# Strassen's seven products in the FFN up-projection of a one-core hybrid decoder layer

## The chip, the cores and the metric

The kernel runs on one core of one Trainium2 chip. The core has five engines with queues of their own, each strictly in order: TensorE (PE in the profile; its weight loads are PEld), VectorE (DVE), ScalarE (ACT), GpSimd (POOL) and SyncE (SP), which here only issues DMAs. They share one on-chip memory, SBUF. TensorE writes its sums to PSUM, of which the FFN uses eight banks; here VectorE and ScalarE read them. The metric is the device time of one execution in microseconds (us).

## The reference

One layer of a hybrid decoder for 2048 prompt tokens and 8 x 4 sample tokens (2080 columns in all), everything in float32. Sliding-window attention and a state space model run side by side, are normed, merged and projected; then comes a gated feed-forward network (FFN) with a short convolution in it:

```
def _conv_ffn(h, prev, w_up, conv_w, conv_b, w_down):
    L = h.shape[1]
    up = h @ w_up
    buf = jnp.concatenate([prev.astype(up.dtype), up], axis=1)
    c = conv_b + sum(conv_w[i] * buf[:, i:i + L] for i in range(CONV_W))
    a, g = jnp.split(c, 2, axis=-1)
    return (jax.nn.silu(g) * a) @ w_down, buf[:, -(CONV_W - 1):]
```

`h` has 1024 features, `up` has 2 x 2688 (value half and gate half), the convolution is three tokens wide, and `w_down` leads back to 1024 features. A last norm follows. The sample tokens have their own past rows `prev`, and the last rows of `up` are returned.

## The kernel before, in words

Features lie on the 128 partitions, tokens along the free axis. Each float32 operand of a large matrix product is split into a high part with float32r's bits and the exact rest (`split`: ScalarE casts the high part, line 85; GpSimd or VectorE subtracts it from the source, line 88). A product is three matmuls per 128 x 128 weight block: high x high, high x low, low x high (`mm3`, lines 93 to 95).

The FFN is the last stage, 760 us to the end. It goes over three groups of two token tiles (some 346 columns each, and two columns of context); for each group over 21 pairs of 128 value and 128 gate features (j = 0 to 20). For each j the weights `wur` (two blocks of 128 x 1024) are loaded and split into `wuh` and `wul`, and `w_down`'s 128 rows into `wdh` and `wdl`. `up(ti, j, ws)` then multiplies: for each half 8 feature blocks x 3 matmuls into one PSUM bank, tag `up`, of which there are four. The convolution reads that bank: ScalarE writes cc = w2 x + b (line 1185), VectorE adds the other two taps (lines 1186 and 1187, one input in PSUM, one in SBUF), ScalarE takes the silu of the gate (1204), VectorE multiplies value and gate (1205, both inputs in SBUF), and the result is split into `ah`, `al`. After every third j, `down` multiplies those with w_down in 16 PSUM banks (tag `dn`, three buffers), and VectorE adds each to the running sum `acc` (1223). The down sums are queued in `todo` and issued after a later `up`, so that the activations are ready.

The order on each engine is set when the program is built: a tile scheduler lists the instructions of each engine once, from the order of the code and priorities, and puts semaphores where a tile is reused. At run time each engine takes its own list from the top. A buffer of a tag with n buffers is free for the (n+1)th tile only when the first has been read for the last time. For the FFN these numbers matter: `wur` 2, `wuh` and `wul` 3, `wdh` and `wdl` 4, `ah` and `al` 7, `up` 4 banks, `dn` 3 banks.

## Time and profile before

| what | value |
|---|---|
| time, median of 3 runs | 2242.93 us (2241.89 to 2244.98) |
| span of the profiled execution | 2245.1 us |
| TensorE busy, matmuls | 2137.4 us, 14183 |
| VectorE, ScalarE, GpSimd busy | 1237.0, 930.8, 978.1 us |
| first and last start of an up matmul | 760.1 and 2206.1 us |
| up and down matmuls of the FFN | 6048 and 3024 |
| mean granted TensorE clock | 0.984 |

A row of a group reads: line, engine, operation, output <- inputs (buffer numbers left out), shapes, count | busy us in all, mean ns of one | idle time of the engine just before them, and what ended it. A matmul's duration is longer than the distance to the next one, because matmuls are pipelined; the distance is read from counts in a full stretch. Timeline rows give the start in us from the span's start, the duration, the engine and the instruction.

### The profile page before, as it was taken

The page shows a single profiled execution, that of the slowest core. Times are in us where ns is not written, and L with a number is a line of the kernel's source. Part 1 is how long each engine was busy: PE and PEld are TensorE (multiplying, and loading weights), DVE is VectorE, ACT ScalarE, POOL GpSimd, SP SyncE. Part 2 cuts the span into 40 slices and gives each one's busy share as a digit, 9 for nine tenths or more (in the row PEclk, how much of TensorE's full clock was granted, in tenths as well). Part 3 has the DMA queues.
Part 4 walks back from the last instruction along what each step waited for, and adds up shares of the span by engine and source line. Part 5 has one row for each costly group of instructions (what it writes and reads, how often), then busy time and mean ns, then how long its engine had stood idle before and what let it go on. Part 6 is the DMA issues. An engine that isn't in the chain of part 4 may idle for free.

```text
span 2245.1 us, 37919 instructions
## 1 busy us (share of the span) xinstructions
PE 2137.4 (95%) x14183; PEld 2068.2 (92%) x14183; DVE 1237.0 (55%) x2786; ACT 930.8 (41%) x1970; POOL 978.1 (44%) x1044
## 2 busy tenths in 40 slices
PE   8969999978999999999999899999999999999997
PEld 8967878857999999999998899999999999999997
DVE  8859898357677654444443654333335743333335
ACT  6526554764444434333333632332224532233333
POOL 4857775343444134433334333443325443344332
PEclk9989999989999999999999999999999999999999
DMA  7765434786365632222126442222213422122202
GB/s 232 240 166 144 137 104 125 144 239 197 114 193 180 207 128 85 81 71 66 48 76 82 136 139 63 85 69 73 69 45 123 142 78 72 40 85 85 66 29 52
DMA packets 204807, 253.22 MB, mean 113 GB/s; under 512 B 32952, under 2 KB 177216, under 8 KB 204608
## 3 DMA queue, kind: packets, MB, share of 16 engines
q1 hardware_dynamic: 204624, 250.80, 39.1%
q8 instruction: 112, 1.84, 0.4%
q14 instruction: 71, 0.58, 0.1%
HBM read 188.69 MB, written 57.71 MB: 110 GB/s over the span
## 4 chain that ended last, share of the span: by engine, by line
PE 63%; DVE 1%; DMA 1%; ACT 1%; issue 0%; POOL 0%; DVEq 0%; ACTq 0%
PE up L95 14%; PE up L94 14%; PE up L93 14%; PE dn L94 7%; PE dn L93 7%; PE dn L95 7%; DMA h2s<-h2scr 1%; DVE acc L1238 0%; PE wo L94 0%; PE wo L95 0%; PE wo L93 0%; DVE cc L1205 0%; DVE h2l L88 0%; DVE acc L1223 0%; ACT h2h L85 0%
## 5 line engine op out<-in xcount | busy, mean ns | idle before, releaser
L95 PE MATMUL up<-h2h,wul 128*128 128x348 f32 (+1 forms) x2016 | 651.0, 323 | 1.4 <-POOL wul L88 1.4
L93 PE MATMUL up<-h2h,wuh 128*128 128x348 f32 (+1 forms) x2016 | 648.6, 322 | 1.4 <-ACT cc L1192 1.4
L94 PE MATMUL up<-h2l,wuh 128*128 128x348 f32 (+1 forms) x2016 | 649.9, 322 | 0.0
L1186 DVE SCALAR_TENSOR_TENSOR cc<-up,cw,cc 128x346 f32<-128x346 f32 (+1 forms) x252 | 144.0, 572 | 456.9 <-ACT cc L1185 456.9
L93 PEld LDWEIGHTS up<-h2h,wuh 128*128 128x128 f32 x2016 | 380.2, 189 | 2.1 <-ACT cc L1192 1.7
L95 PEld LDWEIGHTS up<-h2h,wul 128*128 128x128 f32 x2016 | 380.4, 189 | 1.7 <-POOL wul L88 1.7
L94 PEld LDWEIGHTS up<-h2l,wuh 128*128 128x128 f32 x2016 | 378.5, 188 | 0.4
L88 POOL TENSOR_TENSOR wul<-wur,wuh 128x1024 fp32r<-128x1024 f32 x122 | 294.1, 2411 | 151.5 <-ACT wuh L85 145.8
L93 PE MATMUL dn<-ah,wdh 128*128 128x346 f32 (+1 forms) x1008 | 324.9, 322 | 12.9 <-DVE acc L1223 12.9
L94 PE MATMUL dn<-al,wdh 128*128 128x346 f32 (+1 forms) x1008 | 325.7, 323 | 0.7 <-POOL al L88 0.7
L95 PE MATMUL dn<-ah,wdl 128*128 128x346 f32 (+1 forms) x1008 | 324.4, 322 | 0.0
L1223 DVE TENSOR_TENSOR acc<-acc,dn 128x346 f32<-128x346 f32 (+1 forms) x336 | 172.8, 515 | 230.6 <-PE dn L95 229.8
L88 POOL TENSOR_TENSOR wdl<-wdr,wdh 128x1024 fp32r<-128x1024 f32 x62 | 149.2, 2421 | 345.0 <-PE dn L95 329.9
L88 POOL TENSOR_TENSOR al<-cc,ah 128x346 fp32r<-128x346 f32 (+1 forms) x126 | 118.4, 940 | 340.1 <-ACT ah L85 335.2
L1185 ACT ACTIVATE cc<-up,cw 128x346 f32<-128x346 f32 (+1 forms) x252 | 159.3, 633 | 130.3 <-PE up L95 125.0
L85 ACT CAST wdh<-wdr 128x1024 fp32r<-128x1024 f32 x63 | 64.3, 1048 | 339.9 <-PE dn L94 320.8
L93 PEld LDWEIGHTS dn<-ah,wdh 128*128 128x128 f32 x1008 | 191.7, 190 | 14.4 <-DVE acc L1223 14.3
L94 PEld LDWEIGHTS dn<-al,wdh 128*128 128x128 f32 x1008 | 191.1, 190 | 1.1 <-POOL al L88 1.0
L95 PEld LDWEIGHTS dn<-ah,wdl 128*128 128x128 f32 x1008 | 191.9, 190 | 0.0
L85 ACT CAST wuh<-wur 128x1024 fp32r<-128x1024 f32 x126 | 132.2, 1050 | 132.0 <-PE up L94 126.8
L94 PE MATMUL wo<-ml,wo 128*128 128x260 f32 x512 | 147.3, 288 | 2.4 <-POOL ml L88 1.8
L93 PE MATMUL wo<-mh,wo 128*128 128x260 f32 x512 | 149.1, 291 | 0.3 <-ACT mh L85 0.2
(405 smaller groups left out, 4133.5 us busy)
## 6 DMA issues: line engine op xcount, KB each, us to landing
wur<-in_w_up SPq DMA_DIRECT2D x126, 512.0 KB, 3.6
wdr<-in_w_down SPq DMA_DIRECT2D x63, 512.0 KB, 4.1
x<-in_xT SPq DMA_DIRECT2D x56, 256.0 KB, 3.8
mt<-mscr SPq DMA_DIRECT2D x16, 520.0 KB
xm<-in_xT SPq DMA_DIRECT2D x64, 130.0 KB, 3.0
x2scr<-xm SPq DMA_DIRECT2D x64, 130.0 KB, 2.0
h2scr<-h SPq DMA_DIRECT2D x64, 130.0 KB, 2.6
loscr<-hl_p SPq DMA_DIRECT2D x28, 256.0 KB, 4.4
```

What stands on the lines that cost most here:

```text
L85: nc.scalar.copy(hi, src)
L88: lo_eng.tensor_tensor(lo, src, hi.bitcast(F32), ALU.subtract)
L93: nc.tensor.matmul(ps, w[0], x[0], start=first, stop=False)
L94: nc.tensor.matmul(ps, w[0], x[1], start=False, stop=False)
L95: nc.tensor.matmul(ps, w[1], x[0], start=False, stop=last)
L1185: nc.scalar.activation(cp, pp[:, 2:], AF.Identity, bias=w[3], scale=w[2])
L1186: nc.vector.scalar_tensor_tensor(cp, pp[:, 1 : npr + 1], w[1], cp, ALU.mult, ALU.add)
L1223: nc.vector.tensor_tensor(x[:, m, :n], x[:, m, :n], pt[:, :n], ALU.add)
```

## The change

The FFN's up-projection of one j is a 2 x 2 block product: two feature halves of the weights (value v, gate g) against two token tiles, each cut into two halves of 512 features. It is now done in seven products of 512 features (Winograd's form of Strassen's algorithm) where it had been eight. A product is 4 feature blocks x 3 matmuls of 348 or 350 columns.

- The right-hand sums and differences of the tokens (`x0`, `q0`, `q1`, `t2`) are built once per group in `load_first` and `load_rest`: four VectorE operations for each of four feature blocks, and splits.
- The left-hand sums of the weights are built for every j in `load_wup`: `s1` = g1 + g2 and the first half of `s24` on VectorE, the second half of `s24` and g1 = v1 - g1 (in place) on GpSimd. Then 3.5 blocks of 1024 columns (tags v, s, g, t) are split where it had been 2. The low parts are GpSimd's.
- `unit` runs the seven products. Four of them add up one after another in one PSUM bank (`ux`, two buffers); after each of the first three ScalarE copies the running sum out (c11, c12, u3), and the chain's next product waits for that copy. The other three (u2, u3, u4) go to two banks of tag `up` and are added by VectorE, which also makes the two differences. Of the four results three now lie in SBUF (c11 and c21 in tile `ca`, c12 in `cb`), one in PSUM.
- `conv` does the convolution of a tile as before, but reads those results.
- `down` runs after every second j (11 times a group, before 7), between the fourth and fifth product of the unit that follows the pair. It is called the middle sum below.
- Buffers: `wdh`, `wdl` 3 (before 4), `ah`, `al` 5 (before 7), tiles of 350 columns, `wur` 2 and `wuh`, `wul` 3 as before, though a unit now uses four of the latter and not two. The samples' tails go out by two small DMAs per j, their past rows come by one.

```diff
-TILESF = [(0, 316, NSMP)] + [(348 + 346 * i, 346, 0) for i in range(4)] + [(1732, 348, 0)]
+TILESF = [(0, 316, NSMP), (348, 348, 0)] + [(696 + 346 * i, 346, 0) for i in range(4)]
-AB, WB = 7, 4
+AB, WB, DB_, CB = 5, 3, 2, 6
+SQ = (1, 1)
-        psu, psu_close = psum("fpu", 4)
+        psx, psx_close = psum("fpx", 2)
+        psu, psu_close = psum("fpu", 2)
...
+            for k in range(4):
+                b0 = stage(c2, "c2", gi, 0, k, 4, "hb0")
+                b1 = stage(c2, "c2", gi, 1, k, 4, "hb1")
...
+                v.tensor_tensor(b11, b12, b11, ALU.subtract)
+                v.tensor_tensor(t2, b22, b11, ALU.subtract)
+                v.tensor_tensor(b12, b22, b12, ALU.subtract)
+                v.tensor_tensor(b21, b21, t2, ALU.subtract)
...
+            def pair(src, nm):
+                n = src.shape[1]
+                h = wp.tile([P, KD, P], F32R, tag="wuh", name=f"wh{nm}_{gi}_{j}", bufs=3)[:, 0:n]
+                l = wp.tile([P, KD, P], F32R, tag="wul", name=f"wl{nm}_{gi}_{j}", bufs=3)[:, 0:n]
+                split(nc, h, l, src, nc.scalar, lo_eng)
+                return [[t[:, i : i + 4] for t in (h, l)] for i in range(0, n, 4)]
+            a11, a12 = pair(v, "v")
...
+            nc.vector.tensor_tensor(s1, g[:, 0:4], g[:, 4:8], ALU.add)
+            nc.vector.tensor_tensor(s24[:, 0:4], s1, v[:, 0:4], ALU.subtract)
+            (nc.vector, nc.gpsimd)[SQ[0]].tensor_tensor(s24[:, 4:8], v[:, 4:8], s24[:, 0:4], ALU.subtract)
+            s2, s4 = pair(s24, "s")
+            (nc.vector, nc.gpsimd)[SQ[1]].tensor_tensor(g[:, 0:4], v[:, 0:4], g[:, 0:4], ALU.subtract)
+            s3, a22 = pair(g, "g")
+            (s1,) = pair(s1, "t")
...
-                for k in range(KD):
-                    mm3(nc, pt[:, : n + 2], [w[:, k, :] for w in ws[half]],
-                        (hh[:, k, : n + 2], hl[:, k, : n + 2]), k == 0, k == KD - 1)
...
+            product(chain, a11, b11)
+            nc.scalar.copy(c11, x)
+            p = one("u2")
+            product(p, a12, b21)
+            nc.vector.tensor_tensor(c11, c11, p[:, :w], ALU.add)
+            product(chain, s2, ffn.t2, False)
+            nc.scalar.copy(c12, x)
+            p = one("u3")
+            product(p, s4, b22)
+            nc.vector.tensor_tensor(c12, c12, p[:, :w], ALU.add)
+            if mid:
+                mid()
+            product(chain, s3, q3, False)
+            nc.scalar.copy(u3, x)
+            p = one("u4")
+            product(p, a22, q4)
+            nc.vector.tensor_tensor(c21, u3, p[:, :w], ALU.add)
+            nc.vector.tensor_tensor(c12, c12, u3, ALU.subtract)
+            product(chain, s1, q1, False)
+            conv(t0, j, (c11, c21), prev)
+            nc.vector.tensor_tensor(c12, c12, x, ALU.add)
+            conv(t1, j, (c12, x), None)
...
-                if j % 3 == 2:
+                elif j % 2:
+                    todo.append(lambda g=(t0, t1), w=wds: down(g, w))
```

Where the instructions stand is shown on three engines around unit j = 10 of the second token group. A name ends in group or tile, j and a serial number. On VectorE before, the work of a token tile for one j (`cc_2_10`) was this; `up` is a PSUM bank:

```order
L1186 SCALAR_TENSOR_TENSOR cc_2_10_0_17918<-up_2_10_0_17893,cw_11124,cc_2_10_0_17918 128x346
L1187 SCALAR_TENSOR_TENSOR cc_2_10_0_17918<-up_2_10_0_17893,cw_11124,cc_2_10_0_17918 128x346
L1186 SCALAR_TENSOR_TENSOR cc_2_10_1_17947<-up_2_10_1_17922,cw_11124,cc_2_10_1_17947 128x346
L1187 SCALAR_TENSOR_TENSOR cc_2_10_1_17947<-up_2_10_1_17922,cw_11124,cc_2_10_1_17947 128x346
L1205 TENSOR_TENSOR cc_2_10_0_17918<-cc_2_10_0_17918,cc_2_10_1_17947 128x346
```

Now, after the middle sum (`ca` and `cb` are SBUF tiles, `u4` and `ux` PSUM banks; L1237 and L1238 are the two taps, L1256 the product with the gate):

```order
L1306 TENSOR_TENSOR cb_1_10_18477<-cb_1_10_18477 128x348
L1305 TENSOR_TENSOR ca_1_10_18476<-cb_1_10_18477,u4_1_10_18673 128x348
L1237 SCALAR_TENSOR_TENSOR cc_2_10_18700<-ca_1_10_18476,cw_11124,cc_2_10_18700 128x346
L1309 TENSOR_TENSOR cb_1_10_18477<-cb_1_10_18477,ux_1_10_18475 128x348
L1238 SCALAR_TENSOR_TENSOR cc_2_10_18700<-ca_1_10_18476,cw_11124,cc_2_10_18700 128x346
L1237 SCALAR_TENSOR_TENSOR cc_3_10_18714<-cb_1_10_18477,cw_11124,cc_3_10_18714 128x346
L1256 TENSOR_TENSOR cc_2_10_18700<-cc_2_10_18700 128x346
L1238 SCALAR_TENSOR_TENSOR cc_3_10_18714<-cb_1_10_18477,cw_11124,cc_3_10_18714 128x346
L1237 SCALAR_TENSOR_TENSOR cc_3_10_18714<-ux_1_10_18475,cw_11124,cc_3_10_18714 128x346
L1293 TENSOR_TENSOR ca_1_11_18760<-ca_1_11_18760,u2_1_11_18775 128x348
L1256 TENSOR_TENSOR cc_3_10_18714<-cc_3_10_18714 128x346
L1190 TENSOR_TENSOR s1_1_12_18891<-wur_1_12_1_18885 128x512
```

The taps of three of the four halves now have both inputs in SBUF, and the sums of the weights (s1, here of unit 12) stand behind the convolution in the same queue.

On ScalarE, at the same place, the copies out of the chain's bank (L1290 and L1302) stand between the convolution's steps (L1236 and L1255), which wait for VectorE:

```order
L1302 COPY cb_1_10_18477<-ux_1_10_18475 128x348
L87 CAST whs_1_11_18740<-s24_1_11_18736 128x1024
L1236 ACTIVATE cc_2_10_18700<-ca_1_10_18476,cw_11124 128x346
L87 CAST whg_1_11_18745<-wur_1_11_1_18729 128x1024
L1236 ACTIVATE cc_3_10_18714<-cb_1_10_18477,cw_11124 128x346
L1255 ACTIVATE cc_2_10_18700<-cc_2_10_18700 128x346
L1236 ACTIVATE cc_3_10_18714<-ux_1_10_18475,cw_11124 128x346
L1290 COPY ca_1_11_18760<-ux_1_11_18759 128x348
L87 CAST ah_2_10_18709<-cc_2_10_18700 128x346
L87 CAST wht_1_11_18749<-s1_1_11_18735 128x512
L1255 ACTIVATE cc_3_10_18714<-cc_3_10_18714 128x346
L87 CAST ah_3_10_18723<-cc_3_10_18714 128x346
```

The copy c11 of unit 11 (L1290), for which TensorE's third product of that unit waits, stands behind the silu of unit 10 (L1255); before, no copy of this kind existed.

GpSimd's list between two middle sums began like this before (`wdl`, `wul` low parts of weights, `al` of activations):

```order
L88 TENSOR_TENSOR wdl_1_11_18036<-wdr_1_11_18033,wdh_1_11_18035 128x1024
L88 TENSOR_TENSOR wul_1_10_1_17884<-wur_1_10_1_17881,wuh_1_10_1_17883 128x1024
L88 TENSOR_TENSOR wdl_1_12_18182<-wdr_1_12_18179,wdh_1_12_18181 128x1024
L88 TENSOR_TENSOR wul_1_11_0_18024<-wur_1_11_0_18021,wuh_1_11_0_18023 128x1024
L88 TENSOR_TENSOR al_3_9_17872<-cc_3_9_0_17836,ah_3_9_17871 128x346
L88 TENSOR_TENSOR al_2_10_17954<-cc_2_10_0_17918,ah_2_10_17953 128x346
```

and now, for unit 11 and the start of unit 12:

```order
L90 TENSOR_TENSOR wdl_1_11_18756<-wdr_1_11_18753,wdh_1_11_18755 128x1024
L90 TENSOR_TENSOR wdl_1_12_18912<-wdr_1_12_18909,wdh_1_12_18911 128x1024
L90 TENSOR_TENSOR wls_1_11_18741<-s24_1_11_18736,whs_1_11_18740 128x1024
L90 TENSOR_TENSOR wlg_1_11_18746<-wur_1_11_1_18729,whg_1_11_18745 128x1024
L90 TENSOR_TENSOR al_2_10_18710<-cc_2_10_18700,ah_2_10_18709 128x346
L90 TENSOR_TENSOR wlt_1_11_18750<-s1_1_11_18735,wht_1_11_18749 128x512
L90 TENSOR_TENSOR al_3_10_18724<-cc_3_10_18714,ah_3_10_18723 128x346
L1194 TENSOR_TENSOR wur_1_12_1_18885<-wur_1_12_0_18883,wur_1_12_1_18885 128x512
L1192 TENSOR_TENSOR s24_1_12_18892<-wur_1_12_0_18883,s24_1_12_18892 128x512
L90 TENSOR_TENSOR wlv_1_12_18888<-wur_1_12_0_18883,whv_1_12_18887 128x1024
```

Four blocks of 1024 columns now stand in a row, and wlv, which the next unit's first product reads, comes after two operations on weights (L1194, L1192) that wait for the load of `wur`, whose buffer wlg frees.

More of the change, by code (lines that the diff above doesn't have):

```diff
@@ L1139, in load_wup @@
         def load_wup(gi, j):
[L1140 removed]
+            lo_eng = nc.vector if gi == 0 and j == 0 else nc.gpsimd
+            raws = []
             for half in range(2):
[L1142 to L1147 removed]
@@ L1207, in up, with unit, product, one @@
             al = tp.tile([P, NM], F32R, tag="al", name=f"al_{ti}_{j}", bufs=AB)
-            split(nc, ah[:, :n], al[:, :n], ca[:, :n], nc.scalar, nc.gpsimd)
+            split(nc, ah[:, :n], al[:, :n], ca, nc.scalar, nc.gpsimd)
             acts[ti, j] = (ah, al)
-        def down(grp, wds, between=None):
-            for ti in grp:
+        def unit(gi, j, ws, mid=None):
+            w = WF[gi]
+            t0, t1 = FGROUPS[gi]
+            a11, a12, s2, s4, s3, a22, s1 = ws
+            half = lambda ts, i: [t[:, i] for t in ts]
+            b11, b21 = [t[:, 0:4] for t in ffn.x0], [t[:, 4:8] for t in ffn.x0]
+            (q1, q4), (q3, b22) = [[half(ts, i) for i in range(2)] for ts in (ffn.q0, ffn.q1)]
+            prev = None
+            if TILESF[t0][2]:
+                prev = tp.tile([P, 2, 2 * DB], F32, tag="prev", name=f"prev_{j}")
+                nc.sync.dma_start(prev, cprev[:, :, j])
+            def product(pt, x, y, start=True):
+                for k in range(4):
+                    for i, (p, q) in enumerate(((0, 0), (0, 1), (1, 0))):
+                        nc.tensor.matmul(pt[:, :w], x[p][:, k], y[q][:, k, :w], start=start and k + i == 0,
+                                         stop=k == 3 and i == 2, skip_group_check=True)
+            def one(nm):
+                return psu.tile([P, 512], F32, tag="up", name=f"{nm}_{gi}_{j}")
+            chain = psx.tile([P, 512], F32, tag="ux", name=f"ux_{gi}_{j}")
+            x = chain[:, :w]
+            ca, cb = (c2.tile([P, 2, NM], F32, tag="c2", name=f"c{i}_{gi}_{j}") for i in "ab")
+            c11, c21, c12, u3 = ca[:, 0, :w], ca[:, 1, :w], cb[:, 0, :w], cb[:, 1, :w]
+            product(chain, a11, b11)
[20 more added lines that the diff above has]
+            conv(t1, j, (c12, x), None)
@@ L1213, in down @@
+        def down(tis, wds, between=None):
+            for ti in tis:
                 n = sum(TILESF[ti][1:])
@@ L1267, in body @@
                 wdl = tp.tile([P, D], F32R, tag="wdl", name=f"wdl_{gi}_{j}", bufs=WB)
-                split(nc, wdh, wdl, wr, nc.scalar, nc.vector if gi == 0 and j == 0 else nc.gpsimd)
+                split(nc, wdh, wdl, wr, nc.scalar, nc.gpsimd)
                 wds[j] = (wdh, wdl)
-                for i, ti in enumerate(grp):
-                    up(ti, j, ws)
-                    if j == 0:
+                last = j == NF - 1
+                unit(gi, j, ws, todo.pop(0) if todo and not last else None)
+                if j == 1:
+                    for ti in (t0, t1):
                         load_acc(ti)
-                    if j == NF - 1 and gi + 1 < len(FGROUPS):
-                        load_h2(FGROUPS[gi + 1][i], (ha, hb)[i])
-                    if todo:
-                        todo.pop(0)()
-                if j % 3 == 2:
-                    if j == NF - 1:
-                        last_down(grp, wds)
-                    else:
-                        todo.append(lambda g=grp, w=wds: down(g, w))
+                if last:
+                    if gi + 1 < len(FGROUPS):
+                        load_first(gi + 1, c2, "c2")
+                        load_rest(gi + 1)
+                    while todo:
+                        todo.pop(0)()
+                    down((t0,), wds)
+                    s0 = final_sums(t0)
+                    if gi + 1 < len(FGROUPS):
+                        down((t1,), wds)
+                        s1 = final_sums(t1)
+                        todo += [lambda t=t0, s=s0: final(t, s), lambda t=t1, s=s1: final(t, s)]
+                    else:
+                        with after_preload():
+                            down((t1,), wds, lambda: final(t0, s0))
+                            final(t1, final_sums(t1))
+                elif j % 2:
+                    todo.append(lambda g=(t0, t1), w=wds: down(g, w))
                     wds = {}
-        while todo:
-            todo.pop(0)()
         nc.sync.dma_start(a["o_tail"][:, :, 0:2], tailp)
-        nc.sync.dma_start(a["o_tail"][:, :, 2:], tails)
         tp_close()
         hb_close()
+        c2_close()
         ha_close()
+        sp_close()
         st.wp_close()
@@ L1294, in body @@
         psu_close()
+        psx_close()
 def constants():
```

130 lines of the change are left out of this document (67 added, 63 removed).

## The prediction

> **What bounds the kernel now.** I read the busy times first, then the groups of the FFN, a window inside it, and TensorE's waits.
>
> ```profile
> span 2245.1 us, 37919 instructions
> PE 2137.4 (95%) x14183; PEld 2068.2 (92%) x14183; DVE 1237.0 (55%) x2786; ACT 930.8 (41%) x1970; POOL 978.1 (44%) x1044
> L95 PE MATMUL up<-h2h,wul 128*128 128x348 f32 (+1 forms) x2016 | 651.0, 323 | 1.4 <-POOL wul L88 1.4
> 1300.00:1700.00 400.00, 400.00 (x2510) 400.00 (x2509) 156.53 (x275) 127.41 (x192) 156.77 (x87) 1.00 0.26 77
> PE dn L93 <- DVE acc L1223: 12.9, 5, 10.4
> ```
>
> TensorE sets the pace. In 400 us inside the FFN it started 2510 matmuls with no gap: one every 0.1594 us (the 323 ns is a matmul's own length, they overlap). VectorE, ScalarE and GpSimd were busy for 157, 127 and 157 us of the 400. The only large wait in the FFN is at the change of groups. So a matmul less is 0.16 us less, as long as the other engines keep out of the way; whether they do is the whole question. For that I looked at what VectorE's operations take:
>
> ```profile
> L1186 DVE SCALAR_TENSOR_TENSOR cc<-up,cw,cc x252: 534/578/582, 774.1 to 2207.3; 128x346 f32<-128x346 f32 x84, 128x316 f32<-128x316 f32 x21, 128x348 f32<-128x348 f32 x21
> L1205 DVE TENSOR_TENSOR cc<-cc,cc x126: 507/523/2727, 783.2 to 2209.1; 128x346 f32<-128x346 f32 x84, 128x348 f32<-128x348 f32 x42
> L1201 DVE SCALAR_TENSOR_TENSOR cc<-prev,cw,cc x84: 219/227/2295, 777.3 to 1220.2; 128x8 f32<-128x8 f32 x42, 128x16 f32<-128x16 f32 x42
> L88 POOL TENSOR_TENSOR wul<-wur,wuh x122: 2371/2402/2678, 776.8 to 2188.5; 128x1024 fp32r<-128x1024 f32 x122
> 1347.30 2.40 POOL L88 TENSOR_TENSOR wul<-wur,wuh 128x1024 fp32r<-128x1024 f32 x1
> 1348.60 1.47 DVE L1205 TENSOR_TENSOR cc<-cc,cc 128x346 f32<-128x346 f32 x1 [0.56 <-ACT cc L1204]
> ```
>
> The tap L1186 reads PSUM and SBUF: never above 582 ns. L1205 and L1201 (past rows) read SBUF twice: usually 0.52 and 0.23 us, at times 2.7 and 2.3. The two timeline rows show why. GpSimd's subtraction runs from 1347.30 to 1349.70; L1205 starts at 1348.60 and ends at 1350.07, 0.37 after it: it waited out GpSimd's operation, and only then did its own 346 columns. GpSimd, when second, is late by up to 0.28 (2678 against 2402). **Two-SBUF operations of VectorE and all of GpSimd's exclude each other.** Before, two such VectorE operations per j (L1205) were exposed, far from TensorE.
>
> **The change, part by part.** *Removed:* per unit 7 x 12 = 84 matmuls in place of 96, so 63 x 12 = 756. Columns stay the same. 756 x 0.1594 = **-120.5 us**. The list of TensorE's instructions is shorter by just 756 rows, so this is certain.
>
> *Added.* Durations:
>
> ```profile
> L88 POOL TENSOR_TENSOR wul<-wur,wuh 128x1024 fp32r<-128x1024 f32 x122 | 294.1, 2411 | 151.5 <-ACT wuh L85 145.8 <-issue 4.2
> L88 POOL TENSOR_TENSOR al<-cc,ah 128x346 fp32r<-128x346 f32 x84 | 79.1, 941 | 251.9 <-ACT ah L85 247.1 <-PE up L95 4.9
> L318 POOL TENSOR_TENSOR bb<-b,ff 128x512 f32<-128x512 f32 x1 | 1.3, 1345 | 0.0
> L1223 DVE TENSOR_TENSOR acc<-acc,dn 128x346 f32<-128x346 f32 x224 | 115.3, 515 | 155.4 <-PE dn L95 155.2
> L88 DVE TENSOR_TENSOR wdl<-wdr,wdh 128x1024 fp32r<-128x1024 f32 x1 | 1.2, 1226 | 0.0
> L85 ACT CAST wuh<-wur 128x1024 fp32r<-128x1024 f32 x123 | 129.1, 1049 | 127.6 <-PE up L94 126.8
> L1185 ACT ACTIVATE cc<-up,cw 128x346 f32<-128x346 f32 x168 | 107.0, 637 | 111.9 <-PE up L95 107.3 <-POOL al L88 4.6
> L1204 ACT ACTIVATE cc<-cc 128x346 f32<-128x346 f32 x84 | 41.5, 494 | 98.0 <-DVE cc L1187 97.9
> wur<-in_w_up SPq DMA_DIRECT2D x126, 512.0 KB, 3.6
> ```
>
> Per unit GpSimd now has 3 x 2.4 (v, s, g) + 2.4 (w_down) + 3 x 1.3 (t and two sums of 512) + 2 x 0.94 = 15.4 us, before 3 x 2.4 + 1.9 = 9.1. VectorE has five more sums in or around PSUM (0.52), two weight sums of 512 (0.6), and 8.4 down sums where it had 5.3. Eleven of its operations read SBUF twice: s1, s24, L1306, six taps, two gate products. The shared time of an exclusion is about 0.37 us for 346 columns. TensorE needs 84 + 48 down = 132 matmuls, 21.0 us a unit. So no engine is full; the loss must come from order. The new waits: TensorE's chain waits for a ScalarE copy that stands behind the silu of the unit before; that silu waits for VectorE's taps; these wait for GpSimd's block of 1024; and s1 waits for a load that starts when GpSimd's wlg is done (3.6 us and 0.15 for issue), with VectorE's taps and down sums queued behind it.
>
> I lay the lists out from these durations for one pair of units without and with a middle sum (group 2 or 3; 0 is the end of the middle sum in unit 10; a product is 1.91 us, a PSUM result is there 0.2 after the next product could start: a matmul's 323 ns less the 159, and a hand-over of 0.05):
>
> | us | what |
> |---|---|
> | 1.3 to 11.8 | GpSimd: wdl, wdl, wls, wlg of unit 11; the three gaps between go to VectorE operations |
> | 6.3, 9.0, 11.8 | where L1237 (c21), L1238 (c21), L1237 (c12) each get past one of these blocks |
> | 9.4 to 11.0 | silu after that L1238, last tap's start, then copy c11: product 3 of unit 11 wanted it at 9.6: **1.5 lost** |
> | 15.1 to 17.0 | gate product waits for wlt (to 15.5), then ah, then copy c12: product 5 wanted it at 14.9: **2.1 lost** |
> | 18.1 to 23.75 | load, s1, s24, L1194, L1192, wlv of unit 12, alternating with taps; its first product wanted wlv at 23.1: **0.7 lost** |
> | 23.75, 26.5, 29.2 | L1306, L1237, L1238 get past wlv, wls, wlg |
> | 29.6 to 31.2 | silu, tap, copy c11: product 3 of unit 12 wanted it at 27.3: **4.0 lost** |
> | 34.3 to 40.8 | s1, s24, two taps, L1298 (past al, L1194, L1192), then the first down sum; with three `dn` banks the fourth down product wanted it at 37.9: **2.9 lost** |
>
> Together 11.2 us per pair. The middle sum then gives everything time to catch up, so each pair starts alike. In ten pairs of two groups: 20 x 11.2 = **+224 us**. In group 1 each unit has eight more small VectorE operations for the samples (L1201's kind, 0.23 and more), all now SBUF twice and all ahead of the silu; laid out the same way the losses are 5.8, 0.5, 8.4 and 4.5: 10 x 19.2 = **+192 us**.
>
> Bounds of these terms: if the exclusion costs nothing, the same layout leaves 2.7 us per pair (wlv late by 0.85, the first down sum by 1.85 through the load), 81 us in all, because DMA, s1, L1194, L1192 and wlv follow each other anyway. If every hand-over were 0.1 us slower, some forty of them in a pair's chain add 4 us. I take the layout as it is, since it uses the row that shows the case (1348.60) as it stands.
>
> *Changes of group and start.* VectorE builds the token sums between the down sums: 24 x 0.52 + 16 x 0.52 + 4 x 0.52 + 4 x 0.93 = 27 us against 168 matmuls, 26.8 us, and GpSimd's six blocks of 696 may block it for 0 to 11 us more; the last norm's VectorE work falls into a queue that TensorE now waits for. I take 15 for each change, 10 for the start (0 to 30 each), less the 13 us waited before: **+27 us** (-13 to +77).
>
> *At nothing:* the copies themselves (0.5 of ScalarE per product, covered by the 1.91 us product beside them; without that cover they are the losses above), the samples' DMAs, and all before 760 us, where TensorE's list is the same.
>
> Sum against the profiled span: 2245.1 - 120.5 + 224 + 192 + 27 = 2568; the median lies 2 below the span: **2565 us**.
>
> **The rivals.**
>
> *Faster (queue order alone).* The exclusion falls where VectorE has time to spare, and only the 2.7 us stay: 2245.1 - 120.5 + 81 + 10 = 2215. For it: before, L1205 was blocked in one unit of three without any wait on TensorE. Against: there the silu chain had seven `ah` buffers and four `up` banks of slack; now copy c11 is behind it, with 1.9 us. It decides below 2.8 us lost per pair (120.5 - 27 or so over 30).
>
> *Capacity only.* GpSimd's blocks shift a little and the waits merge; what is left is the shared time outside the middle sums: GpSimd 30.8 less the 8.2 it does in them (al, wlt, al, L1194, L1192, wlv), plus VectorE's 18 x 0.37 + 4 x 0.55, is 31 us, where TensorE has 26.8: 4 us a pair, 2245 - 120.5 + 30 x 4 + 27 = 2270.
>
> *Clock.*
>
> ```profile
> 1228.00:1238.50 10.50, 2.28 (x15) 2.00 (x13) 0.00 (x0) 0.00 (x0) 0.00 (x0) 0.81 1.24 88
> 1238.50:1246.00 7.50, 5.30 (x22) 5.30 (x23) 6.39 (x11) 5.53 (x11) 2.61 (x2) 0.58 0.67 230
> ```
>
> After the one gap of 10 us the granted clock was 0.58 for 7.5 us. If the 8.4 us losses of group 1 do the same, each costs some 5 us more (10 of them): 2615. [...]
>
> [...]
>
> **How the numbers follow.** Layout as it stands 0.55 (own range 2440 to 2695, its 416 us less or more by 30%); clock as well 0.1; capacity only 0.15; faster 0.17; the rest, worse still, 0.03. Range 2205 to 2700. Within 0.2% (4.5 us, about what can be told from no change) lies only the border between capacity and faster: 0.03. Faster by more 0.17, slower by more 0.80.
>
> **What would show it.** Right: TensorE busy well below 95% in the FFN; waits of `ux` matmuls for ScalarE's `ca` copies and of `dn` for `acc` at the head of the list; taps L1237/L1238 with a mean far above 0.58 us in the forms that read `ca` and `cb`, and at 0.58 from `ux`; group 1 the slowest of three. Wrong: taps at 0.58 throughout (exclusion absent), or no waits on TensorE (time to spare); then it is near 2215. If the waits of `ux` are for GpSimd's `wl` tiles, the load and order, and not the exclusion, are the cause.

## The result, and the profile after

The changed kernel takes **2571.3 us** (median of 4 runs, 2571.25 to 2573.98) against 2243.45 (median of 4 runs, 2241.89 to 2244.98): a ratio of **1.1467, 95% interval 1.1451 to 1.1483**. The forecast was slower, 2565 us. The head of the profile page (span, busy times, and TensorE's granted clock in 40 slices):

```profile
span 2572.2 us, 38054 instructions
PE 2148.3 (84%) x13427; PEld 2041.1 (79%) x13427; DVE 2023.5 (79%) x3482; ACT 1105.9 (43%) x2263; POOL 1473.2 (57%) x1307
PEclk9989999899997888888898799999998799999997
DVE 33%; PE 31%; ACT 5%; issue 4%; DMA 2%; POOL 1%; SPq 0%; DVEq 0%; POOLq 0%; ACTq 0%
DVE cc L1237 8%; PE ux L1279 8%; DVE cc L1238 8%; PE dn L95 5%; PE u L1279 5%; PE dn L97 5%; PE dn L96 5%; DVE cc L1253 4%; DVE s L1191 2%; ACT cc L1236 2%; DVE cb L1306 2%; ACT cc L1255 1%; DVE acc L1339 1%; PE wo L96 1%; DVE cc L1256 1%
```

TensorE ran 756 matmuls less (13427 against 14183), but it is busy 84% of the span instead of 95%. The last two rows are the chain of work that ended last, by engine and by line: VectorE now has the largest part, 33%, where before it had 1% and TensorE 63%, and the two taps L1237 and L1238 stand near its head. What TensorE's up and down products wait for (us in all, times, the longest), all rows above 3 us:

```profile
PE ux L1279 <- ACT ca L1290: 241.3, 63, 28.8
PE dn L95 <- DVE acc L1324: 48.8, 37, 5.3
PE ux L1279 <- ACT cb L1295: 27.1, 18, 1.6
PE ux L1279 <- POOL wlv L90: 3.5, 18, 0.4
```

Each of the 63 units waits once for ScalarE's copy c11 (L1290): that is the chain's second link, product 3. The taps, by what they read (minimum, median and maximum in ns):

```profile
L1237 DVE SCALAR_TENSOR_TENSOR cc<-ca,cw,cc x126: 534/1474/2801, 799.7 to 2522.1; 128x346 f32<-128x346 f32 x84, 128x316 f32<-128x316 f32 x42
L1238 DVE SCALAR_TENSOR_TENSOR cc<-ca,cw,cc x126: 533/1495/2721, 800.3 to 2522.8; 128x346 f32<-128x346 f32 x84, 128x316 f32<-128x316 f32 x42
L1238 DVE SCALAR_TENSOR_TENSOR cc<-ux,cw,cc x63: 564/577/580, 817.9 to 2528.0; 128x346 f32<-128x346 f32 x42, 128x348 f32<-128x348 f32 x21
```

The same tap takes 0.58 us when it reads PSUM (`ux`) and 1.5 us in the median, up to 2.8, when it reads SBUF (`ca`). The taps that read `cb`, in SBUF too, take 0.57 to 0.58 in the median and up to 2.7: what counts as well is whether GpSimd is at work when they start. Of the 63 L1237 from `cb`, 18 started under a GpSimd operation and took 2.68 to 2.70 us, the others at most 0.58; of the 63 L1238, 21 did and took 0.81 to 1.23, the others again at most 0.58. A piece of the timeline after a middle sum, at the start of unit 11 of group 2, VectorE and GpSimd first, then ScalarE (start, duration, engine; idle time before it in brackets):

```profile
1705.95 2.78 POOL L90 TENSOR_TENSOR wls<-s,whs 128x1024 fp32r<-128x1024 f32 x1
1706.82 2.29 DVE L1238 SCALAR_TENSOR_TENSOR cc<-ca,cw,cc 128x346 f32<-128x346 f32 x1
1708.69 2.65 POOL L90 TENSOR_TENSOR wlg<-wur,whg 128x1024 fp32r<-128x1024 f32 x1
1709.04 2.69 DVE L1237 SCALAR_TENSOR_TENSOR cc<-cb,cw,cc 128x346 f32<-128x346 f32 x1
...
1709.15 0.50 ACT L1255 ACTIVATE cc<-cc 128x346 f32<-128x346 f32 x1 [1.41 <-DVE cc L1238]
1709.55 0.62 ACT L1236 ACTIVATE cc<-ux,cw 128x346 f32<-128x346 f32 x1
1710.07 0.44 ACT L1290 COPY ca<-ux 128x348 f32<-128x348 f32 x1
```

The tap L1238 starts at 1706.82 under GpSimd's block `wls` and ends at 1709.11, 0.38 us after the block's end (1708.73). Silu (L1255) waits for it, and copy c11 (L1290) stands behind silu.

**Where the time went.** From the starts of the matmuls in the trace I count, for each unit, how far TensorE fell behind one matmul per 0.16 us: distances above 0.4 us as waits, the rest as slow matmuls.

| stretch | waits | slow matmuls | together |
|---|---|---|---|
| start (unit 0 of group 1) | 34.0 | 3.4 | 37.4 |
| units 1 to 19 of group 1 | 102.5 | 45.8 | 148.4 |
| units 3 to 19 of groups 2 and 3 | 118.6 | 28.8 | 147.4 |
| changes of group (unit 20, then units 0 to 2) | 98.4 | 19.4 | 117.9 |
| end (unit 20 of group 3) | 17.6 | 2.4 | 19.9 |
| all | 371.2 | 99.8 | 471.0 |

Before, the same count gave 20.7 in all. So the FFN's first to last matmul went from 1473.9 to 1803.3 us: 756 matmuls fewer, at 0.16 us each, are -121.0, and 471.0 - 20.7 = +450.3.

### The profile page after: what moved, and what is told of

It is laid out like the page before. It is cut to its first block, busy times and chain, and to the rows that moved or that the text cites. A ratio compares the mean times of both kernels' runs of the same rounds, so it can differ in the third digit from the quotient of the medians.

```text
span 2572.2 us, 38054 instructions
## 1 busy us (share of the span) xinstructions
PE 2148.3 (84%) x13427; PEld 2041.1 (79%) x13427; DVE 2023.5 (79%) x3482; ACT 1105.9 (43%) x2263; POOL 1473.2 (57%) x1307
## 4 chain that ended last, share of the span: by engine, by line
DVE 33%; PE 31%; ACT 5%; issue 4%; DMA 2%; POOL 1%; SPq 0%; DVEq 0%; POOLq 0%; ACTq 0%
DVE cc L1237 8%; PE ux L1279 8%; DVE cc L1238 8%; PE dn L95 5%; PE u L1279 5%; PE dn L97 5%; PE dn L96 5%; DVE cc L1253 4%; DVE s L1191 2%; ACT cc L1236 2%; DVE cb L1306 2%; ACT cc L1255 1%; DVE acc L1339 1%; PE wo L96 1%; DVE cc L1256 1%
## 5 line engine op out<-in xcount | busy, mean ns | idle before, releaser
L1324 DVE TENSOR_TENSOR acc<-acc,dn 128x346 f32<-128x346 f32 (+1 forms) x528 | 265.5, 513 | 166.6 <-PE dn L97 166.6
L1279 PE MATMUL ux<-t2h,whs 128*128 128x348 f32 (+1 forms) x252 | 110.1, 437 | 243.8 <-ACT ca L1290 241.3
L1279 PEld LDWEIGHTS ux<-t2h,whs 128*128 128x128 f32 x252 | 62.7, 249 | 262.2 <-ACT ca L1290 259.3
L1237 DVE SCALAR_TENSOR_TENSOR cc<-ca,cw,cc 128x346 f32<-128x346 f32 (+1 forms) x126 | 172.6, 1370 | 59.3 <-ACT cc L1236 58.8
L1238 DVE SCALAR_TENSOR_TENSOR cc<-ca,cw,cc 128x346 f32<-128x346 f32 (+1 forms) x126 | 192.9, 1531 | 2.1
L90 POOL TENSOR_TENSOR wls<-s,whs 128x1024 fp32r<-128x1024 f32 x62 | 164.8, 2658 | 28.4 <-ACT whs L87 28.4
L90 POOL TENSOR_TENSOR wlv<-wur,whv 128x1024 fp32r<-128x1024 f32 x62 | 158.8, 2561 | 15.1 <-ACT whv L87 14.3
L90 POOL TENSOR_TENSOR wlg<-wur,whg 128x1024 fp32r<-128x1024 f32 x62 | 161.7, 2609 | 0.3 <-ACT whg L87 0.3
L95 PE MATMUL wo<-mh,wo 128*128 128x260 f32 x512 | 147.8, 289 | 0.2 <-ACT mh L87 0.2
L97 PE MATMUL wo<-mh,wo 128*128 128x260 f32 x512 | 145.6, 284 | 0.0
L1255 ACT ACTIVATE cc<-cc 128x346 f32<-128x346 f32 (+1 forms) x126 | 62.2, 494 | 183.1 <-DVE cc L1238 96.4
L1194 POOL TENSOR_TENSOR wur<-wur,wur 128x512 f32<-128x512 f32 x63 | 104.3, 1656 | 61.2 <-DVE s L1190 61.2
```

Source lines behind the costliest of these rows:

```text
L90: lo_eng.tensor_tensor(lo, src, hi.bitcast(F32), ALU.subtract)
L95: nc.tensor.matmul(ps, w[0], x[0], start=first, stop=False)
L97: nc.tensor.matmul(ps, w[1], x[0], start=False, stop=last)
L1194: (nc.vector, nc.gpsimd)[SQ[1]].tensor_tensor(g[:, 0:4], v[:, 0:4], g[:, 0:4], ALU.subtract)
L1237: nc.vector.scalar_tensor_tensor(cp, pp[:, 1 : npr + 1], w[1], cp, ALU.mult, ALU.add)
L1238: nc.vector.scalar_tensor_tensor(cp, pp[:, 0:npr], w[0], cp, ALU.mult, ALU.add)
```

## The experiments

The theory: VectorE's operations with two SBUF inputs wait out GpSimd's blocks, and TensorE waits for what stands behind them. The rivals: VectorE simply has too much work; a copy stands in the wrong place of ScalarE's list; the clock. Each time is compared with the kernel before on the same chip: 2250.7 us for the runs without low parts, with cut blocks, with silu behind the copy and with the low parts on VectorE; 2240.0 for those with taps from PSUM, with a third load buffer, with silu behind the copy and the low parts on VectorE together, and without the samples' operations; 2246.0 for the next three (all sums on VectorE, one block given back, no last norm). The change itself is **+328** over the runs of before that stand beside it. All but the last version are single runs, so a few us tell nothing.

**Without the low parts of the weights.**

```diff
-                l = wp.tile([P, KD, P], F32R, tag="wul", ...)[:, 0:n]
-                split(nc, h, l, src, nc.scalar, lo_eng)
-                return [[t[:, i : i + 4] for t in (h, l)] for i in range(0, n, 4)]
+                nc.scalar.copy(h, src)
+                return [[t[:, i : i + 4] for t in (h, h)] for i in range(0, n, 4)]
```

> Leaves out the low parts of the up weights: GpSimd's four subtractions a unit (blocks v, s, g, t; 8.5 us) are gone, and the matmuls that used them read the high part again, so TensorE, VectorE and ScalarE have the same instructions as in the change. Theory (VectorE's two-SBUF operations wait out GpSimd's blocks, and TensorE waits for what stands behind them): taps that read ca and cb fall from a mean of 1.3 to 1.7 us to below 0.8 us; a pair of units in groups 2 and 3 loses at most 2.5 us instead of 8.9; time 2200 to 2280. Rival (VectorE simply has too much work, or ScalarE's copies stand in the wrong place, whatever GpSimd does): taps may fall, the pairs keep losing 6 us or more, time above 2450. Rival (TensorE's lower clock): time falls only by the 100 us of matmuls at half rate, to some 2470.

2260.7 us, **+10** over before. A window over eight pairs of group 2 (columns: the window, its length, then busy time and count of TensorE's matmuls, its weight loads, VectorE, ScalarE and GpSimd, granted clock, DMA share, GB/s):

```profile
1374.30:1712.00 337.70, 337.70 (x2114) 337.70 (x2113) 237.50 (x400) 157.01 (x257) 122.36 (x80) 1.00 0.25 75
```

The pairs of groups 2 and 3 lose nothing; those of group 1 lose 24 in all where they lost 148. The taps that read `ca` fall from 1.37 and 1.53 us in the mean to 0.59 and 0.88 (the second misses the theory's 0.8). The theory's mechanism holds, and neither VectorE's own work nor the order of its list stops TensorE by itself. But the run is not faster than before: start 37.6, changes 80.0 and end 14.4 us are still there, 132 us that eat the whole 121. This run takes GpSimd's time away together with the exclusion, so it doesn't tell the two apart. The next run does.

**Taps from PSUM, GpSimd unchanged.**

```diff
-            p = one("u2")
+            p = p2 = one("u2")
...
-            conv(t0, j, (c11, c21), prev)
+            conv(t0, j, (c11, c21) if prev else (p2[:, :w], p[:, :w]), prev)
```

> In groups 2 and 3 the four taps of the first token tile read the banks of u2 and u4 in PSUM where they read c11 and c21 in SBUF. Every engine has the same instructions in the same order, and GpSimd's blocks stay as they are; what is left out is that c11 and c21 do not go into the convolution there. Theory (it is the second SBUF input that lets GpSimd's block hold up the tap): these taps take 0.57 us each, the waits of product 3 in units with a middle sum fall from 3.4 to below 1.5 us, pairs of groups 2 and 3 lose 3 to 6 us instead of 8.9, group 1 stays; time 2460 to 2530. Rival (VectorE has too much to do, or the lists' order is at fault): same counts, same order, so the same time within 15 us of 2575.

2499.6 us, **+260**, within the theory's range. First the changed kernel's groups of VectorE in units 3 to 20 of group 2, then this run's (count, busy time, mean ns):

```profile
L1238 DVE SCALAR_TENSOR_TENSOR cc<-ca,cw,cc 128x346 f32<-128x346 f32 x34 | 64.0, 1883 | 0.6
L1256 DVE TENSOR_TENSOR cc<-cc 128x346 f32<-128x346 f32 x34 | 27.2, 799 | 2.8
```

```profile
L1238 DVE SCALAR_TENSOR_TENSOR cc<-u,cw,cc 128x346 f32<-128x346 f32 x35 | 20.1, 574 | 0.6
L1256 DVE TENSOR_TENSOR cc<-cc 128x346 f32<-128x346 f32 x36 | 66.8, 1856 | 2.5
```

With the same instructions in the same order (a few sums at the changes of group apart), the tap falls from 1883 to 574 ns because its first input lies in PSUM. GpSimd's blocks still run beside it: between 1500 and 2450 us, 36 of the 78 taps L1238 start under a GpSimd operation of over 2 us and take 0.57; in the changed kernel 34 of 72 do, and take 2.2 to 2.3. The pairs of groups 2 and 3 lose 5.7 and 5.0 us instead of 8.9, and product 3 waits no more in them. So it is the second SBUF input. The second row shows why not all is won: the block now catches the next operation with two SBUF inputs, the gate product L1256.

**GpSimd's blocks cut.** The expectation speaks of two pieces of 512; the kernel that ran cuts the blocks into four of 256.

```diff
+CUT = 2
...
-                split(nc, h, l, src, nc.scalar, lo_eng)
+                nc.scalar.copy(h, src)
+                for i in range(0, n, CUT):
+                    lo_eng.tensor_tensor(l[:, i : i + CUT], src[:, i : i + CUT], h[:, i : i + CUT].bitcast(F32), ALU.subtract)
```

> GpSimd's subtractions of 1024 columns are made as two of 512 (some 1.3 us each instead of 2.4 to 2.6); nothing else changes. Theory (a VectorE operation waits out the one GpSimd operation that is under way): no wait for a weight block above some 1.4 us, TensorE's losses about halved, time 2400 to 2480. Rival (what counts is GpSimd's time in all, not the length of one operation): the same or slower, 2565 to 2620, since two halves take about 0.2 us more than one block.

2603.6 us, **+353**: slower than the change, in the rival's range. The pairs of group 1 did get shorter (57.9 to 54.8 us), but those of groups 2 and 3 grew from 51.1 to 54.7. The theory was right on the single wait (beside the short pieces the taps take 1.0 to 1.1 us in the timeline) and product 3's wait in groups 2 and 3 fell from 3.4 to below 1.0. But GpSimd pays: its pieces, and VectorE's and TensorE's new waits:

```profile
L1187 POOL TENSOR_TENSOR wls<-s,whs 128x256 fp32r<-128x256 f32 x64 | 63.7, 1025 | 0.0
L1187 POOL TENSOR_TENSOR wlt<-s,wht 128x256 fp32r<-128x256 f32 x32 | 22.9, 736 | 0.0
DVE s L1193 <- DMA wur<-in_w_up: 165.7, 39, 5.4
PE dn L96 <- DVE acc L1327: 127.9, 39, 5.9
```

Four pieces of `wls` take 4.1 us, where one block took 2.7. I read this as VectorE coming between the pieces. GpSimd is later, the load of w_up that needs its tile is later, s1 (L1193 here) waits for the load, and the down sums queue behind s1: 7 us per pair at the down sums, where it had been about one.

With a third buffer for that load:

> The run with cut blocks again (it cut them into four of 256 columns), with a third buffer for the loads of w_up and one buffer instead of two for w_down's. In that run the wait of product 3 had gone, but VectorE waited 4.2 to 4.9 us for the load of w_up, and the down sums behind it on VectorE 7 us. Theory (the load starts when the block that reads the old tile is done, and cut blocks are done later): with the third buffer the down sums' wait falls below 2.5 us per pair, time 2400 to 2500. Rival (GpSimd's longer work in all sets the pace; it was busy 312 of 437 us): the wait moves to wl tiles, time stays above 2560.

```diff
-AB, WB, DB_, CB = 5, 3, 2, 6
+AB, WB, DB_, CB = 5, 3, 1, 6
...
-                r = wp.tile([P, KD, P], F32, tag="wur", ...)
+                r = (wp.tile([P, KD, P], F32, tag="wur", ...) if (2 * (NF * gi + j) + half) % 3 else
+                     sp.tile([P, KD, P], F32, tag="wu3", ..., bufs=1))
```

2623.6 us, **+384**: the theory of the load fails. The wait for the load is gone, and another is in its place:

```profile
DVE s L1194 <- POOL wlt L1188: 126.5, 55, 4.3
PE dn L96 <- DVE acc L1328: 104.5, 44, 4.9
```

s1 has one buffer, and the block `wlt`, the last block of weights in GpSimd's list for a unit, reads the old one. So with cut blocks it is GpSimd's list as a whole that is late, as the rival had it, by way of `wlt` and not of the load. (w_down's load had one buffer less in this run; what that cost isn't separated.)

**The order on ScalarE.** Silu and what follows are issued behind the next unit's copies, first with GpSimd as it is, then with the low parts on VectorE.

```diff
-            nc.scalar.copy(c11, x)
+            copied = nc.scalar.copy(c11, x)
+            if gates:
+                with tc.issue_after(copied.ins):
+                    gates.pop(0)()
...
-            conv(t0, j, (c11, c21), prev)
+            gates.append(conv(t0, j, (c11, c21), prev))
```

(The same stands at c12 and at the second tile; `conv` ends before silu and returns the rest.)

> Silu, gate product and split of a unit are issued behind the next unit's copies of c11 and c12, so that these copies no longer stand behind a silu on ScalarE. GpSimd's blocks stay. If the place of the copy behind the silu is what costs (the mechanism that the forecast named), product 3's wait of 3.4 us in units with a middle sum and 0.8 without, and product 5's 1.6, mostly go: time 2400 to 2470. If VectorE, held up by GpSimd's blocks, sets the pace of a pair whatever the order on ScalarE, the wait turns up elsewhere (two up banks, three dn banks, or the same product behind other work): time 2540 to 2600.

2644.1 us, **+393**, above both ranges. Where TensorE waits:

```profile
PE ux L1282 <- ACT ca L1293: 200.4, 45, 28.8
PE dn L95 <- DVE acc L1333: 111.7, 41, 5.3
```

In group 3 product 3's wait falls from 3.5 to 1.0 and from 0.8 to nothing. In its place product 7 waits 2.2, and the fourth down product 4.7 instead of 0.65. The copy's place sets where TensorE waits, but not how much: the waits went elsewhere and grew. That VectorE's list beside GpSimd's sets the amount fits this, but the run doesn't show it by itself.

> Low parts of the up weights on VectorE, and silu behind the next unit's copies, both together. Theory (the copy's place decides only once VectorE is not held up): pairs lose less than 1.5 us instead of 3.3 to 4.1 with the first edit alone, time 2260 to 2310, beside 2343. Rival (the order with silu first is the better one whatever GpSimd does): 2343 to 2420, as the second edit alone was 60 to 70 us slower.

2387.9 us, **+148**, against +92 for the low parts on VectorE alone (next). So this order is worse by itself: the pairs' product 3 waits 1.4, but the down sums wait 2.9. The gate product is now issued later in VectorE's list, and the theory that the copy's place would decide once VectorE is free falls. Which of the moved operations costs the down sum is not settled.

**Work moved from GpSimd to VectorE.**

```diff
-            lo_eng = nc.vector if gi == 0 and j == 0 else nc.gpsimd
+            lo_eng = nc.vector
```

> The four low parts of the up weights move from GpSimd to VectorE (3 x 1.23 + 0.62 = 4.3 us a unit, by the one block of 1024 that VectorE subtracted before in 1226 ns). VectorE's own work goes from some 14 to 18.5 us a unit of 21; GpSimd keeps w_down, the activations and two sums (7 us). Theory (exclusion): taps below 0.8 us on average, pairs lose at most 4 us, time 2220 to 2330. Rival (too much work on VectorE is the cause): the pairs become longer by the 8.6 us that VectorE gets, time above 2700.

2342.6 us, **+92** where the change has +328, though 13 above the theory's range. VectorE got 4.3 us more work per unit, and the pairs became shorter, from 51.1 to 45.5 and 46.3 us. Then the two weight sums as well:

```diff
-SQ = (1, 1)
+SQ = (0, 0)
```

> Low parts of the up weights on VectorE, and the second half of s24 and g1 = v1 - g1 too (0.62 us each by VectorE's sums of 512, on GpSimd 1.5 to 1.75); GpSimd keeps w_down's and the activations' low parts. Theory (each GpSimd operation taken away frees VectorE of a wait): pairs lose less than with the low parts alone (3.3 and 4.1 us), time 2290 to 2335. Rival (VectorE, busy 82% there, is now the bound itself): pairs get longer, time above 2345.

2283.2 us, **+37**, below the theory's range. Units 4 to 19 of group 2:

```profile
1365.20:1717.20 352.00, 342.86 (x2115) 337.54 (x2114) 300.09 (x497) 157.55 (x257) 74.59 (x48) 1.00 0.23 72
L90 DVE TENSOR_TENSOR wlg<-wur,whg 128x1024 fp32r<-128x1024 f32 x16 | 19.4, 1215 | 0.0
L1194 DVE TENSOR_TENSOR wur<-wur,wur 128x512 f32<-128x512 f32 x16 | 10.8, 677 | 0.0
```

VectorE is busy 300 of 352 us and TensorE loses only 1.8 us per pair: too much work on VectorE is not the cause. VectorE does the block in 1.2 us where GpSimd took 2.4 to 2.7, and the sum in 0.68 where GpSimd took 1.74. By the count of the table TensorE still loses 34.3 us in the start, 92.6 in the changes, 15.3 at the end and 44 in all pairs, more than the 121 us that the matmuls left out save.

> As the run with all sums on VectorE, but the block v of every odd j goes back to GpSimd: it falls into the middle sum of the unit before, where VectorE's operations read PSUM. Theory (GpSimd's blocks cost nothing there): VectorE has 1.2 us less per pair and no new waits, time 5 to 35 us below that run. Rival (the block runs into the taps behind the middle sum or ahead of it): 5 to 40 us above that run.

```diff
-                split(nc, h, l, src, nc.scalar, lo_eng)
+                split(nc, h, l, src, nc.scalar, nc.gpsimd if nm == "v" and j % 2 else lo_eng)
```

2314.1 us, **+68**: the rival. The run with one block given back to GpSimd in every second unit is 31 us longer. Only 24 of them lie in the FFN (1542.4 us from its first to its last matmul, 1518.8 without); its first matmul starts 7 us later, which the edit doesn't explain. The middle-sum units of group 2 grow from 30.25 to 31.4, with a new wait of 1.1 us at the down sums.

**The samples of group 1.**

```diff
-                    for wi, dst, src in (
-                        (1, cs[:, :, 1:4], us[:, :, 0:3]),
...
-                    ):
+                    for wi, dst, src in ():
```

> Leaves out the samples' eight small VectorE operations a unit in group 1 (the convolution of the sample tokens keeps only its first term). Theory (they are what makes group 1 slower than groups 2 and 3, as each may be held up by a block of GpSimd): pairs of group 1 fall from 57.9 us to 50 to 53, group 1 from 651 us to 570 to 600, time down by 50 to 80. Rival (group 1 is slower because of TensorE's lower clock or because of the samples' DMAs): pairs stay above 55 us.

2510.7 us, **+271**. Pairs of group 1 go from 57.8 to 51.1 us, just what groups 2 and 3 take, and the group from 650.6 to 592.1. First the changed kernel over units 1 to 19 of group 1, then this run over the same units:

```profile
808.00:1350.00 542.00, 449.19 (x2462) 441.30 (x2461) 439.51 (x619) 200.50 (x342) 303.45 (x171) 0.89 0.19 56
```

```profile
808.00:1287.70 479.70, 417.88 (x2462) 406.65 (x2461) 377.44 (x466) 199.45 (x341) 310.74 (x170) 0.96 0.22 63
```

The clock rose from 0.89 to 0.96 without being touched: in group 1 the low clock follows from the waits and is not what starts them.

**The changes of group.**

```diff
         def final_sums(ti):
+            if ti not in FGROUPS[-1]:
+                return None
...
+                if ss:
                     nc.vector.scalar_tensor_tensor(x, x, g_fin[:, k : k + 1], r, ALU.mult, ALU.mult)
```

> Leaves out the last norm of the first two groups (their sums of squares and the scaling of acc; those output columns stay unscaled), which VectorE does in the first three units of the next group: 16 sums and 16 scalings of 0.5 us at least, the eight scalings of a tile 7.1 us in one stretch between two taps. Theory (these lie in VectorE's queue ahead of the tap that silu and copy c11 wait for, and TensorE now waits there): product 3 of the first three units of groups 2 and 3 waits 3 to 6 us instead of 9.5, 11.7 and 11.9; time 35 to 60 us less, 2510 to 2540. Rival (the first units of a group wait for the new tokens' sums or loads): these waits stay above 9 us, time above 2560.

2523.7 us, **+278**. Product 3 of the first three units waits 2.7, 2.3 and 6.4 us in group 2 and 0, 2.6 and 2.7 in group 3; the changes cost 70.1 us instead of 117.9. So the last norm is 48 us of them. The run also leaves out ScalarE's part of the norm, and the 6.4 us in group 2 stay unexplained. What stands in the way in the changed kernel, on VectorE and then on ScalarE:

```profile
1435.83 7.12 DVE L1339 SCALAR_TENSOR_TENSOR acc<-acc,vec,rs_fo 128x348 f32<-128x348 f32 x8
1442.87 0.57 DVE L1238 SCALAR_TENSOR_TENSOR cc<-ca,cw,cc 128x346 f32<-128x346 f32 x1
1444.45 0.68 ACT L1236 ACTIVATE cc<-cb,cw 128x346 f32<-128x346 f32 x1 [7.34 <-DVE cb L1309]
```

Eight scalings stand between the two taps. ScalarE waits 7.34 us for the sum L1309, which stands behind them on VectorE, and silu and copy c11 stand behind that L1236. A last version tried to keep the norm and hide it, on the best kernel so far:

```diff
-            conv(t1, j, (c12, x), None)
+            tap = conv(t1, j, (c12, x), None)
+            if late:
+                with tc.issue_after(tap.ins):
+                    late.pop(0)()
...
-            ... nc.gpsimd if ti == FGROUPS[-1][1] else nc.vector)
+            ... nc.gpsimd if ti % 2 else nc.vector)
```

(`late` holds the eight scalings of a tile; the second line is the engine of the sums of squares.)

> As the run with all sums on VectorE (2283 us), and in the first two groups the last norm's scalings are issued behind the last tap of their unit instead of between two taps, and the second tile's sums of squares go to GpSimd, which is idle then. Theory (what stands ahead of the tap in VectorE's queue is what the group change costs; behind it, it is covered): product 3 of the first three units of groups 2 and 3 waits below 3 us each instead of 6.2, 6.5, 8.9 and 3.3, 6.6, 7.2; time 2248 to 2268. That would still not be below the kernel before, as the start (31 us), the sums of the tokens at the changes (14 us each) and 1 to 2 us per pair remain. Rival (the scalings then hold up the sum of u2 and the weight sums behind them): 2272 to 2295.

2281.5 us (median of 4) against 2246.1 (median of 7): **1.0163, interval 1.0146 to 1.0180**. In time there is next to no gain beside the run with all sums on VectorE (2283.2). The trace shows one in the FFN: 1511.6 us against 1518.8 from its first to its last matmul, 84.8 against 92.6 in the changes; but here the FFN starts 5 us later, for a reason that the edit doesn't explain. The scalings did move: product 3 of unit 1 waits 3.2 and 2.9 us instead of 6.5 and 6.6. But unit 0 waits 9.2 and 5.7 instead of 6.2 and 3.3, for the sums of squares that I gave to GpSimd:

```profile
1278.87 7.94 POOL L125 TENSOR_TENSOR ss_fo<-ss_fo,sq_fo 128x348 f32<-128x348 f32 x6 [0.40 <-ACT sq_fo L124]
1280.62 1.94 DVE L90 TENSOR_TENSOR wlg<-wur,whg 128x1024 fp32r<-128x1024 f32 x1
1282.48 3.54 DVE L125 TENSOR_TENSOR ss_fo<-ss_fo,sq_fo 128x348 f32<-128x348 f32 x3
```

VectorE's `wlg` takes 1.94 us instead of 1.22, and three sums of 0.5 take 3.54, beside those six sums. GpSimd was idle there, but its work is not free for VectorE. No version here beats the kernel before.

## Why the prediction was right, and where it was not

**Removed, -120.5.** Right: 756 matmuls are gone, and where nothing waits TensorE starts one every 0.16 us, as in the run without low parts (2114 in 337.7 us).

**The exclusion.** Right. No row that the forecast read shows a tap over all columns held up like the old L1205; that it would be was my estimate. The run with taps from PSUM shows it by the home of one operand alone (1883 against 574 ns). The 1706.82 row shows it for one tap, 2.29 us where 0.58 is its time alone. Counted over the FFN (from 760 us), VectorE's operations on two tensors that start under a GpSimd operation with over 0.3 us to go: before, 50 have no PSUM input, and all 50 end after it; 308 have one, and none takes over 0.58 us. In the changed kernel 454 of 457 without a PSUM input end after it. The other three ended first, and there it is GpSimd's L1194 that is late: 2.51 and 2.09 us, where its median is 1.74.

**The laid-out pair.** Right in kind at each place, about a quarter too long in all. The waits alone, without the slow matmuls that the forecast put at nothing, are 6.9 us where it had 11.2. Lost us in a pair of group 3, forecast and measured:

| place | forecast | measured |
|---|---|---|
| product 3 without a middle sum (copy c11) | 1.5 | 0.8 |
| product 5 (copy c12) | 2.1 | 1.6 |
| first product (wlv) | 0.7 | 0.3 |
| product 3 with a middle sum | 4.0 | 3.5 |
| fourth down product | 2.9 | 0.6 |
| slow matmuls | 0 | 2.0 |
| pair | 11.2 | 8.9 |

The fourth down product was the term most mis-sized. The layout's 0.05 for a hand-over and 0.15 for an issue were estimates of mine: in the trace of before VectorE starts 0.03 us after the ScalarE operation that it waits for, and a load of w_up is issued 0.03 after the block that frees its buffer. A pair of group 1 was put at 19.2 and measured 15.6: 4.8 and 4.3 at product 3 (5.8 and 8.4 in the forecast), 1.7 at the down sum (4.5), nothing at product 5 (0.5), and 4.8 of slow matmuls (nothing). That it is the samples' small operations is shown by the run without them. The bound "without exclusion 2.7 per pair" was not met as such: in groups 2 and 3 the run without low parts lost nothing, but it took GpSimd's work away too, and with it the late start of the load that s1 would have waited for.

**Changes of group and start, +27.** This step was wrong. The table's start, changes and end measured 37.4 + 117.9 + 19.9 = 175.2, less the 20.7 of before: +154.5. These stretches hold seven units that the forecast counted in its pairs, for 43 us, so +27 stands for +70 here and its upper bound of 77 for 120. On the same stretches:

| stretch | forecast | measured |
|---|---|---|
| units 1 to 19 of group 1 | 182 | 148 |
| units 3 to 19 of groups 2 and 3 | 190 | 147 |
| changes of group | 68 | 118 |
| start and end | 16 | 57 |
| less the same in the kernel before | -13 | -21 |
| all | 443 | 450 |

So the total came out right by luck: two errors of 77 and 84 us met. I had counted VectorE's token sums beside the down matmuls and taken 15 per change. Missing at the changes was the last norm in the first three units (48 us, by the run without it), which I named but did not price by the place where it stands, between two taps. The start was put at 10. There product 3 waits 34 us, 28.8 of it at once for copy c11:

```profile
774.49 1.23 DVE L90 TENSOR_TENSOR wls<-s,whs 128x1024 fp32r<-128x1024 f32 x1 [3.32 <-ACT whs L87]
781.98 5.55 POOL L90 TENSOR_TENSOR wdl<-wdr,wdh 128x1024 fp32r<-128x1024 f32 x2
782.68 2.65 DVE L1162 TENSOR_TENSOR hb<-hb,hb 128x350 f32<-128x350 f32 x1
785.44 2.47 DVE L1163 TENSOR_TENSOR ht<-hb,hb 128x350 f32<-128x350 f32 x1
787.95 0.49 ACT L87 CAST t2h<-ht 128x350 fp32r<-128x350 f32 x1 [6.19 <-DVE ht L1163]
789.74 0.45 ACT L1290 COPY ca<-ux 128x350 f32<-128x350 f32 x1
```

TensorE had ended product 2 at 761.4. The low part `wls`, which product 3 reads too, is ready at 775.72, so about half of the 28.8 us would have been lost without any copy: the weights of this product are sums now, and these take until then. In the other half the copy stands on ScalarE behind the casts of the token sums; the cast waits for VectorE's sums of 0.5 us, which take 2.65 and 2.47 beside GpSimd's blocks of w_down. That is the same mechanism at a place that I had not laid out. How much of the start it makes up, no run separates: none took w_down's blocks from GpSimd.

**The rivals.** *Faster, 2215*: in the run without low parts the pairs of groups 2 and 3 lose nothing, and it still came to +10, since the start, the changes and the end cost 132 us there. The rival's chance of 0.17 rested on the undersized term. *Capacity only, 2270*: too small, as it had 4 us a pair where 8.9 and 15.6 were measured. With VectorE busy 300 of 352 us TensorE is almost free (all sums on VectorE), so VectorE's own capacity is not it. But the rival counted the time that GpSimd's work and VectorE's two-SBUF operations need together, and that run takes GpSimd's work away. With cut blocks GpSimd's list as a whole was late. So a part of the loss may be this shared time, and no run separates it from the order. *Clock*: half true. The clock was lower (0.89 over group 1, in the row above), and slow matmuls make up 100 us of the table: 2.4 us a unit in group 1, where the rival had 5 after each loss of 8.4, and 1.7 us a pair in groups 2 and 3, which its 2615 doesn't count. But a part of it costs nothing. Two middle-sum units of group 2, each with its wait and what follows it:

```profile
1726.30:1729.60 3.30, 0.25 (x2) 0.00 (x0) 3.23 (x4) 1.81 (x4) 1.64 (x1) 1.00 0.23 48
1729.60:1731.25 1.65, 1.49 (x9) 1.49 (x10) 1.61 (x4) 1.24 (x4) 1.08 (x2) 1.00 0.56 221
1731.25:1734.67 3.42, 3.42 (x14) 3.42 (x13) 3.25 (x4) 1.67 (x4) 2.45 (x3) 0.50 0.00 0
...
1777.40:1780.70 3.30, 0.19 (x2) 0.00 (x0) 3.23 (x4) 1.80 (x5) 1.61 (x1) 1.00 0.17 31
1780.70:1783.00 2.30, 2.17 (x13) 2.17 (x14) 2.13 (x5) 1.48 (x4) 1.76 (x2) 1.00 0.45 183
```

After the same idle time the clock was 0.50 for 3.42 us in the first and stayed at 1.00 in the second. The first unit took 34.93 us, the second 35.11: where the matmuls are slow (1.76 against 0.41 us lost), the fourth down product waits that much less (0.66 against 2.12). So it is not TensorE that sets the pair's length there. In group 1 it is not so simple: units 16 and 17, with 1.2 to 1.5 us fewer lost to slow matmuls, were 0.6 and 1.2 us shorter than their neighbours. How much of the 100 us is real is not settled.

**What would show it.** All five signs came: TensorE at 84% of the span (82% from its first to its last up matmul), `ux` for `ca` and `dn` for `acc` at the head of the waits, the taps far above 0.58 us in the mean from `ca` (1.37 and 1.53) and less clearly from `cb` (1.18 and 0.78), at 0.58 from `ux`, and group 1 the slowest.
